# Moving subtractions of a sum of rows to GpSimd, a shorter root, and a split last scaling in a fused decoder layer

## The chip, the cores and the metric
The kernel runs on one core of a Trainium2 chip. The metric is the device time in microseconds (us), the median of several executions. The engines are TensorE (PE; its weight loads are listed as PEld), VectorE (DVE), ScalarE (ACT), GpSimd (POOL) and SyncE (SP), whose queue issues the transfers.

## The reference
One layer of a decoder over 16 meta tokens and 1024 tokens of width 1024. Only the second half of it and its norms matter here.

```python
def rmsnorm(x, g):
    x32 = x.astype(jnp.float32)
    y = x32 * lax.rsqrt(jnp.mean(x32 * x32, axis=-1, keepdims=True) + EPS)
    return (y * g.astype(jnp.float32)).astype(x.dtype)

def swiglu(u, w_gate, w_up, w_down):
    return (jax.nn.silu(u @ w_gate) * (u @ w_up)) @ w_down
...
        h = h + hybrid_mixer(rmsnorm(h, attn_norm_g[l]), pos, topk, w_in[l], mla_q_norm_g[l], w_uq[l],
                             mla_kv_norm_g[l], w_ukv[l], w_o[l])
        h = h + swiglu(rmsnorm(h, ffn_norm_g[l]), w_gate[l], w_up[l], w_down[l])
    h = rmsnorm(h, final_norm_g)
    return h[:, N_META:t]
```

The mixer holds two groups of attention heads (one dense, one over the 256 best keys of each query), and an output projection `w_o`. Norms are taken of the input, of two latent vectors, of the sum after the mixer, and of the result.

## The kernel before, in words
The 1024 tokens are eight blocks of 128 rows. Every float32 factor of a product is cut into a high part of fewer bits (written by ACT, `split`, line 188) and a low part, the difference of the factor and its high part (a subtraction on DVE or POOL, lines 191 and 193); a product is three matmuls (lines 196 to 198: high x high, high x low, low x high, in the order that the factors' roles give).

The stages in time order: the input norm and projection; the dense and the sparse attention for blocks 0 to 2 and then 3 to 7; the output projection of blocks 0 to 2 and their feed-forward part, inside the attention of the later blocks; the output projection of blocks 3 to 7 (`out_proj`); the feed-forward part of blocks 3 to 7 (`ffn_sums`); the last norm (`last_norm`) of each block as its last feed-forward sum comes in.

The feed-forward part of blocks 3 to 7 uses a scheme of seven products instead of eight quarter products. It works on sums of row halves and of column halves. `sums_of` writes the seven left factors `us[0]` to `us[6]` for each block from the block's two transposed halves, which lie in PSUM (`x11`, `x12`, `x21`, `x22`, 128 x 256 each); `first_factors` writes the weights' factors. The tiles `wsh` and `wsl` and parts of older tiles (`ckH`, `wkH`) are the slots for the high and low parts of these; of the seven, two low parts are subtracted by DVE and five by POOL.

`out_proj` goes over the blocks with a lag: after a block's projection comes the sum of its squares, the norm's factor (`rstd`, lines 155 to 161: six DVE instructions around one square root on ACT), two scaled halves `un` (line 1069), eight transposes on TensorE (line 1072), and then `put`, the sums of that block (lines 1107 to 1118), one block behind. The first transfers of the feed-forward weights go into four buffers `raw`; a buffer is loaded anew when the last reader of its contents is done.

`rstd` serves all norms: 9 at the input, 17 for the latent vectors, one call for blocks 0 to 2 together (three columns), 5 for blocks 3 to 7 and 8 for the last norm. In the last norm the first half of a block is scaled by DVE with the norm's factor and the weights at once (line 1301), the second half by ACT and then by POOL (lines 1298 and 1299), except for the last block, where DVE scales both halves.

The program text gives the work and what depends on what. In which order each engine's queue takes its instructions is written by a planner that simulates the whole program (`schedule_with_timeline_sim=True`); each queue then runs in that order.

Of the kernel before, what the change touches and what calls it, by code (L numbers as in the profile page):

```python
# [11 lines left out]
F32 = mybir.dt.float32  # L12
# [6 lines left out]
AF = mybir.ActivationFunctionType  # L19
OP = mybir.AluOpType  # L20
# [5 lines left out]
D = 1024  # L26
P = 128
NB = T // P
# [12 lines left out]
EPS = 1e-6  # L41

NA = 3
BLK_A, BLK_B = tuple(range(NA)), tuple(range(NA, NB))
# [33 lines left out]
SEG = P // 2  # L78
NSEG = NB - NA
NPR = 7  # L80
WS_N, RAW_N = 5, 4
# [24 lines left out]
def hybrid_layer(ctx, tc, a, out):  # L106
    nc = tc.nc
    V, S, G, PE = nc.vector, nc.scalar, nc.gpsimd, nc.tensor
    ld = nc.sync.dma_start
# [38 lines left out]
    def bcast_rows(src, n, parts=P):  # L148
        return bass.AP(tensor=src.tensor, offset=src.offset, ap=[[0, parts], [1, n]])

    def rstd(pool, ss, n, parts=P, tag="rs"):

        w = ss.shape[-1]
        v = pool.tile([parts, 4, w], F32, name=tag, bufs=3)
        V.tensor_scalar(v[:, 0], ss, 1.0 / n, EPS, op0=OP.mult, op1=OP.add)
        S.activation(v[:, 1], v[:, 0], AF.Sqrt)
        V.reciprocal(v[:, 1], v[:, 1])
        V.tensor_mul(v[:, 2], v[:, 1], v[:, 1])  # L158
        V.tensor_mul(v[:, 2], v[:, 2], v[:, 0])
        V.tensor_scalar(v[:, 2], v[:, 2], -0.5, 1.5, op0=OP.mult, op1=OP.add)  # L160
        V.tensor_mul(v[:, 3], v[:, 1], v[:, 2])
        return v[:, 3]

    def v_scale(pool, i, bound, rest):
# [21 lines left out]
    def split(h, l, src, eng=None):  # L186

        S.activation(h, src, AF.Copy)  # L188
        if eng is G and len(src.shape) == 2:
            for c in cuts(src.shape[-1], 256):  # L190
                G.tensor_sub(l[:, c], src[:, c], h[:, c])  # L191
        else:
            (eng or V).tensor_sub(l, src, h)  # L193
# [46 lines left out]
    with ExitStack() as es:  # L240
# [29 lines left out]
        def norm_in(src, parts, dst, t=-1):  # L270

            xt = xp.tile([P, D], F32, name="xt", bufs=2)
            ld(xt[:parts], src)
            if parts == NM:
                ld(gb, bcast_rows(a["attn_norm_g"], D))
            ss = xp.tile([P, 1], F32, name="ss", bufs=3)
            S.activation(act_junk()[:parts, :D], xt[:parts], AF.Square, accum_out=ss[:parts])
            r = rstd(xp, ss[:parts], D, parts, tag="rs")
            if t >= XT_G:
                S.activation(xt, xt, AF.Copy, scale=r)  # L280
                G.tensor_mul(xt, xt, gb)
            else:
                V.scalar_tensor_tensor(xt[:parts], xt[:parts], r, gb[:parts], op0=OP.mult, op1=OP.mult)
            for g in range(2):
                pt = ps_t()
                for d in range(4):
                    PE.transpose(pt[:, d * P:d * P + parts], xt[:parts, (g * 4 + d) * P:(g * 4 + d + 1) * P],
                                 ident[:parts, :parts])
                dst(slice(g * 4, g * 4 + 4), pt.rearrange("p (c n) -> p c n", n=P))
# [224 lines left out]
        def latent(dst, src, n, g, parts=P):  # L514
            ss = ip.tile([P, 1], F32, name="ssc", bufs=3)[:parts]
            S.activation(act_junk()[:parts, :n], src, AF.Square, accum_out=ss)
            r = rstd(ip, ss, n, parts, "rsc")
            V.scalar_tensor_tensor(dst, src, r, g[:parts], op0=OP.mult, op1=OP.mult)
# [141 lines left out]
    oh = [op.tile([P, D], F32, name=f"oh{t}") for t in range(NB)]  # L660
# [365 lines left out]
    def out_proj(wo, blocks, load, cw, ot, put, tps, ops, ends, lag=0):  # L1026
# [19 lines left out]
        for c, i in steps:  # L1046
# [15 lines left out]
            tot = wo.tile([P, 4], F32, name="ss2", bufs=2)[:, 0:i + 1 - i0]  # L1062
            V.reduce_sum(tot, ss[:, i0:i + 1], axis=AX.X)
            r = rstd(wo, tot, D, P, "rs2")
            for k in range(i0, i + 1):
                for g in range(2):
# [21 lines left out]
    def sums_of(wo, us):  # L1088

        def ot(i, part, g):
            return us[2 * part + g][:, i].rearrange("p a d n -> p (a d n)").rearrange("p (d n) -> p d n", n=P)

        first = {}

        def put(i, g, pt):
            if not g:
                first[i] = pt
                return  # L1100
            (x11, x12), (x21, x22) = ([x[:, :, j * SEG:(j + 1) * SEG] for j in range(2)] for x in (first.pop(i), pt))
            t0, t1, t2, t3, t4 = (wo.tile([P, 4, SEG], F32, name=f"ts{x}", bufs=1) for x in range(5))

            def parts(k, src, eng=None):
                split(us[k][:, i, 0], us[k][:, i, 1], src, eng)

            S.activation(t0, x11, AF.Copy)
            parts(0, x11)
            V.tensor_sub(t1, x12, t0)
            parts(1, x21)  # L1110
            V.tensor_sub(t2, x22, t1)
            parts(2, t2)
            parts(3, t1, G)
            G.tensor_sub(t3, t2, t0)
            parts(4, t3, G)
            parts(5, x22)
            V.tensor_sub(t4, x21, t2)
            parts(6, t4, G)

        return ot, put  # L1120
# [157 lines left out]
    def last_norm(fu):  # L1278

        gl = fu.tile([P, D], F32, name="gl")  # L1280
        ld(gl, bcast_rows(a["final_norm_g"], D))
        sums = {}

        def half(t, c):
            if not c:
                sums[t] = fu.tile([P, 2], F32, name="ss3", bufs=3)
            S.activation(fu.tile([P, 512], BF, name="yj"), oh[t][:, c * 512:(c + 1) * 512], AF.Square,
                         accum_out=sums[t][:, c:c + 1])
            if not c:
                return  # L1290
            tot = fu.tile([P, 1], F32, name="ss4", bufs=3)
            V.tensor_add(tot, sums[t][:, 0:1], sums[t][:, 1:2])
            r = rstd(fu, tot, D, P, "rs3")
            for k in range(2):
                y = oh[t][:, k * 512:(k + 1) * 512]
                g = gl[:, k * 512:(k + 1) * 512]
                if k and t < NB - 1:
                    S.activation(y, y, AF.Copy, scale=r)
                    G.tensor_mul(y, y, g)
                else:  # L1300
                    V.scalar_tensor_tensor(y, y, r, g, op0=OP.mult, op1=OP.mult)  # L1301
                ld(out[0, t * P:(t + 1) * P, k * 512:(k + 1) * 512], y)

        return half

    def pool(es, name, **kw):
        return es.enter_context(tc.tile_pool(name=name, bufs=1, **kw))
# [7 lines left out]
    with aa_es:  # L1315
        work = attention(aa, BLK_A, cfg)
        rest = mla_rest()
        n = 0
# [42 lines left out]
    fu = pool(fa, "fua")  # L1361
# [14 lines left out]
    for x, y in ((ckH, ckL), (wkH, wkL)):  # L1376
        n = x.shape[1] // WO_W
# [55 lines left out]
```

## Time and profile before
| what | us |
|---|---|
| runs: median (lowest, highest) of 3 | 1507.58 (1507.29, 1510.57) |
| the profiled execution | 1510.57 |
| its span, first to last instruction | 1508.8 |
| TensorE busy | 1403.7 |
| VectorE busy | 1101.3 |
| ScalarE busy | 923.7 |
| GpSimd busy | 893.6 |

The time of an execution holds its span and what lies around it. Busy times overlap. The granted clock is the share of TensorE's full rate that the chip granted; over the whole span it was 0.974.

### The profile page before, as it was taken

Reading aid. Unit: us, or ns where it says so; the run is one execution under the profiler, and the core shown is the slowest. Engines: PE = TensorE matmul, PEld = TensorE weight load, DVE = VectorE, ACT = ScalarE, POOL = GpSimd, SP = SyncE. Lnnn points to the kernel's source line nnn. Section 1 sums busy time; section 2 is a strip of 40 time slices with the busy share of each in tenths; the row PEclk is TensorE's granted clock in tenths of the full one; section 3 lists DMA queues with packets and bytes.
Section 4 is the critical chain, followed back from the end, with each engine's and each line's share of the span. In section 5 each row is a group of like instructions: output and inputs, shape, how many; then the busy total and the mean of one; then the engine's idle time right before and its main releaser. Section 6 shows DMA issues by size and latency. Waiting matters only on the chain. (4 is left out here: it accounts for less than half of the span.)

```text
span 1508.8 us, 29965 instructions
## 1 busy us (share of the span) xinstructions
PE 1403.7 (93%) x10320; PEld 1293.0 (86%) x10320; DVE 1101.3 (73%) x2714; ACT 923.7 (61%) x2264; POOL 893.6 (59%) x1185
## 2 busy tenths in 40 slices
PE   6999998899989799899999999897899999999996
PEld 5999998897879689798888888797899999999995
DVE  5888989948886785966776657647566777777766
ACT  5666678896888889788644444554544444444434
POOL 2573555212405587787878879663846666666653
PEclk9999999999999799999999999998899999999998
DMA  6213365223434788678879998661212222222211
GB/s 172 61 48 87 80 139 133 51 89 115 137 113 114 144 187 174 149 154 182 188 162 199 200 214 193 161 189 39 71 57 84 84 84 84 84 75 80 84 56 70
DMA packets 353737, 180.74 MB, mean 120 GB/s; under 512 B 196560, under 2 KB 341344, under 8 KB 353584
## 3 DMA queue, kind: packets, MB, share of 16 engines
q1 hardware_dynamic: 353584, 178.82, 48.0%
q8 instruction: 81, 1.33, 0.4%
q14 instruction: 72, 0.59, 0.1%
HBM read 120.77 MB, written 21.30 MB: 94 GB/s over the span
## 5 line engine op out<-in xcount | busy, mean ns | idle before, releaser
L191 POOL TENSOR_TENSOR wL<-raw,wH 128x256 fp32r<-128x256 f32 x352 | 286.7, 848 | 60.6 <-ACT wH L188 56.3
L821 POOL TENSOR_TENSOR hl<-pd,hl 128x260 f16<-128x260 f32 (+5 forms) x256 | 168.8, 689 | 70.5 <-ACT hl L817 38.0
L191 POOL TENSOR_TENSOR wsl<-raw,wsh 128x256 fp32r<-128x256 f32 x132 | 120.6, 942 | 95.9 <-ACT wsh L188 48.5
L196 PE MATMUL b<-wh,uH 128*128 128x256 f32 (+3 forms) x568 | 169.3, 298 | 5.1 <-DVE mlo L318 3.2
L198 PE MATMUL b<-wh,uL 128*128 128x256 f32 (+3 forms) x568 | 168.8, 298 | 0.0
L197 PE MATMUL b<-wl,uH 128*128 128x256 f32 (+3 forms) x568 | 168.5, 297 | 0.1
L188 ACT ACTIVATE wH<-raw 128x1024 fp32r<-128x1024 f32 x88 | 91.8, 1055 | 80.8 <-DMA raw<-in_w_gate 20.8
L196 PE MATMUL b<-us,wsh 128*128 128x320 f32 x440 | 136.2, 313 | 1.6 <-ACT us L188 1.0
L197 PE MATMUL b<-us,wsh 128*128 128x320 f32 x440 | 136.5, 311 | 0.4 <-DVE us L193 0.4
L198 PE MATMUL b<-us,wsl 128*128 128x320 f32 x440 | 134.8, 310 | 0.0
L196 PE MATMUL b<-ua,wH 128*128 128x384 f32 x352 | 121.8, 346 | 3.3 <-ACT wH L188 3.3
L382 ACT ACTIVATE js<-sc,bs 128x528 bf16<-128x528 int16 (+7 forms) x128 | 120.9, 944 | 4.8 <-DVE sc L437 2.4
L197 PE MATMUL b<-ua,wH 128*128 128x384 f32 x352 | 121.2, 344 | 0.0
L198 PE MATMUL b<-ua,wL 128*128 128x384 f32 x352 | 121.0, 345 | 0.0
L196 PE MATMUL b<-wH,hH 128*128 128x512 f32 x282 | 113.9, 404 | 4.4 <-ACT hH L188 3.1
L196 PEld LDWEIGHTS b<-wh,uH 128*128 128x128 f32 x568 | 108.8, 192 | 7.2 <-DVE mlo L318 3.9
L197 PE MATMUL b<-wL,hH 128*128 128x512 f32 x282 | 112.5, 399 | 0.0
L198 PE MATMUL b<-wH,hL 128*128 128x512 f32 x282 | 110.2, 400 | 0.4 <-DVE hL L193 0.4
L197 PEld LDWEIGHTS b<-wl,uH 128*128 128x128 f32 x568 | 109.1, 192 | 0.5 <-DVE wl L193 0.3
L198 PEld LDWEIGHTS b<-wh,uL 128*128 128x128 f32 x568 | 109.0, 192 | 0.4 <-DVE uL L193 0.2
L1248 DVE TENSOR_TENSOR oh<-b,oh 128x512 f32<-128x512 f32 x110 | 74.5, 685 | 43.3 <-PE b L198 42.6
L799 ACT ACTIVATE pd<-pd,sm 128x528 f32<-128x528 f32 (+4 forms) x80 | 75.7, 946 | 48.7 <-DVE sm L797 46.0
(410 smaller groups left out, 4834.9 us busy)
## 6 DMA issues: line engine op xcount, KB each, us to landing
raw<-in_w_gate SPq DMA_DIRECT2D x44, 512.0 KB, 4.0
raw<-in_w_up SPq DMA_DIRECT2D x44, 512.0 KB, 4.1
raw<-in_w_down SPq DMA_DIRECT2D x44, 512.0 KB, 3.6
wor<-in_w_o SPq DMA_DIRECT2D x64, 128.0 KB, 2.7
wraw<-in_w_in SPq DMA_DIRECT2D x40, 128.0 KB, 2.5
vh<-v_x SPq DMA_DIRECT2D x16, 288.0 KB, 4.0
xt<-in_x SPq DMA_DIRECT2D x8, 512.0 KB, 4.1
ks_x<-st SPq DMA_DIRECT2D x32, 128.0 KB, 2.2
```

Of the source, the lines that this page charges most:

```text
L188: S.activation(h, src, AF.Copy)
L191: G.tensor_sub(l[:, c], src[:, c], h[:, c])
L196: PE.matmul(o, lh, rh, start=first, stop=False, **kw)
L197: PE.matmul(o, lh, rl, start=False, stop=False, **kw)
L198: PE.matmul(o, ll, rh, start=False, stop=last, **kw)
L382: S.activation(act_junk()[:, :n_keys(b)], y[b], AF.Sign, bias=cols[0], accum_out=cnt)
L799: S.activation(pb, pb, AF.Exp, bias=mn, scale=-1.0, accum_out=z)
L821: G.tensor_sub(pl_[:, c], pb[:, c], ph[:, c])
L1248: V.tensor_add(oh[t][:, cs], po, oh[t][:, cs])
```

## The change
In `put`, the low part of `us[2]` is subtracted by POOL instead of DVE, in all five blocks. For blocks 3 to 6 (not the last) ACT copies `x22` from PSUM into a new tile `ts5`, both parts of `us[5]` are taken from this copy, and the low part is subtracted by POOL.

`rstd` takes -4 (mean + eps), its root with the sign turned in ACT's instruction, the reciprocal, and then one step of refinement in two DVE instructions if there is one column (three if there are more), where it took four.

In the last norm the last block's halves are multiplied by the norm's weights into a buffer of the `raw` ring (DVE: 512 and 256 columns, POOL: 256), ahead of the norm's factor; then DVE scales one half and ACT the other.

```diff
     def rstd(pool, ss, n, parts=P, tag="rs"):
 
+
         w = ss.shape[-1]
         v = pool.tile([parts, 4, w], F32, name=tag, bufs=3)
-        V.tensor_scalar(v[:, 0], ss, 1.0 / n, EPS, op0=OP.mult, op1=OP.add)
-        S.activation(v[:, 1], v[:, 0], AF.Sqrt)
+        V.tensor_scalar(v[:, 0], ss, -4.0 / n, -4.0 * EPS, op0=OP.mult, op1=OP.add)
+        S.activation(v[:, 1], v[:, 0], AF.Sqrt, scale=-1.0)
         V.reciprocal(v[:, 1], v[:, 1])
-        V.tensor_mul(v[:, 2], v[:, 1], v[:, 1])
-        V.tensor_mul(v[:, 2], v[:, 2], v[:, 0])
-        V.tensor_scalar(v[:, 2], v[:, 2], -0.5, 1.5, op0=OP.mult, op1=OP.add)
-        V.tensor_mul(v[:, 3], v[:, 1], v[:, 2])
+        if w == 1:
+            V.scalar_tensor_tensor(v[:, 2], v[:, 1], v[:, 1], v[:, 0], op0=OP.mult, op1=OP.mult)
+        else:
+            V.tensor_mul(v[:, 2], v[:, 1], v[:, 1])
+            V.tensor_mul(v[:, 2], v[:, 2], v[:, 0])
+        V.scalar_tensor_tensor(v[:, 3], v[:, 2], 3.0, v[:, 1], op0=OP.add, op1=OP.mult)
         return v[:, 3]
...
             V.tensor_sub(t2, x22, t1)
-            parts(2, t2)
+            parts(2, t2, G)
             parts(3, t1, G)
             G.tensor_sub(t3, t2, t0)
             parts(4, t3, G)
-            parts(5, x22)
+            if i < len(BLK_B) - 1:
+                t5 = wo.tile([P, 4, SEG], F32, name="ts5", bufs=1)
+                S.activation(t5, x22, AF.Copy)
+                x22 = t5
+            parts(5, x22, G if i < len(BLK_B) - 1 else V)
             V.tensor_sub(t4, x21, t2)
             parts(6, t4, G)
...
             if not c:
                 return
+            if t == NB - 1:
+
+                yg = fu.tile([P, D], F32, name="raw", bufs=RAW_N)
+                V.tensor_mul(yg[:, 0:512], oh[t][:, 0:512], gl[:, 0:512])
+                G.tensor_mul(yg[:, 512:768], oh[t][:, 512:768], gl[:, 512:768])
+                V.tensor_mul(yg[:, 768:], oh[t][:, 768:], gl[:, 768:])
             tot = fu.tile([P, 1], F32, name="ss4", bufs=3)
             V.tensor_add(tot, sums[t][:, 0:1], sums[t][:, 1:2])
             r = rstd(fu, tot, D, P, "rs3")
             for k in range(2):
+                if t == NB - 1:
+                    y = yg[:, k * 512:(k + 1) * 512]
+                    if k:
+                        S.activation(y, y, AF.Copy, scale=r)
+                    else:
+                        V.tensor_scalar(y, y, r, None, op0=OP.mult)
+                    ld(out[0, t * P:(t + 1) * P, k * 512:(k + 1) * 512], y)
+                    continue
                 y = oh[t][:, k * 512:(k + 1) * 512]
                 g = gl[:, k * 512:(k + 1) * 512]
-                if k and t < NB - 1:
+                if k:
                     S.activation(y, y, AF.Copy, scale=r)
                     G.tensor_mul(y, y, g)
                 else:
```

## Rows read from the trace of the kernel before
**Rows 1.** The page: span, and busy time of each engine (x instructions).
```profile
span 1508.8 us, 29965 instructions
...
PE 1403.7 (93%) x10320; PEld 1293.0 (86%) x10320; DVE 1101.3 (73%) x2714; ACT 923.7 (61%) x2264; POOL 893.6 (59%) x1185
```
**Rows 2.** Windows: start:end, length, busy time of each engine; clock, DMA share, GB/s.
```profile
100.00:200.00 100.00, 99.01 (x708) 97.54 (x707) 90.48 (x289) 68.25 (x205) 52.80 (x69) 1.00 0.35 91
1043.40:1061.00 17.60, 6.47 (x26) 4.17 (x27) 16.68 (x41) 9.41 (x30) 10.63 (x13) 0.60 0.09 31
1046.00:1068.80 22.80, 13.15 (x63) 11.13 (x62) 16.94 (x42) 13.40 (x37) 16.58 (x23) 0.63 0.07 24
1057.00:1068.80 11.80, 10.37 (x53) 9.25 (x52) 6.05 (x15) 7.29 (x18) 8.89 (x14) 0.70 0.00 1
1094.80:1474.00 379.20, 379.18 (x2210) 349.07 (x2211) 267.02 (x390) 157.92 (x309) 228.15 (x260) 1.00 0.26 77
```
**Rows 3.** TensorE's waits from 1000 us: who waited, total, times, longest.
```profile
PE b L1072 <- DVE un L1069: 7.1, 2, 3.7
PE b L196 <- ACT hH L188: 3.1, 1, 3.1
PE b L1072 <- DVE rs L160: 1.5, 1, 1.5
```
**Rows 4.** Groups by form, 1030 to 1066 us, and one tile's instructions (min/median/max).
```profile
L193 DVE TENSOR_TENSOR us<-b,us 128x256 fp32r<-128x256 f32 x15 | 6.2, 413 | 1.2 <-ACT us L188 1.2
L193 DVE TENSOR_TENSOR us<-ts,us 128x256 fp32r<-128x256 f32 x5 | 2.8, 551 | 1.0 <-ACT us L188 1.0
...
L193 POOL TENSOR_TENSOR us<-ts,us x15: 724/735/1267, 1033.5 to 1066.7; 128x256 fp32r<-128x256 f32 x15
...
L1107 ACT ACTIVATE ts<-b 128x256 f32<-128x256 f32 x5 | 1.8, 370 | 0.2 <-PE b L1072 0.2
```
**Rows 5.** Timeline of DVE, 1049 to 1056 us: start, length, instruction.
```profile
1050.44 0.88 DVE L193 TENSOR_TENSOR us<-ts,us 128x256 fp32r<-128x256 f32 x1
1051.24 0.41 DVE L193 TENSOR_TENSOR us<-b,us 128x256 fp32r<-128x256 f32 x1
...
1054.58 0.41 DVE L193 TENSOR_TENSOR us<-ts,us 128x256 fp32r<-128x256 f32 x1
1054.91 0.41 DVE L193 TENSOR_TENSOR us<-b,us 128x256 fp32r<-128x256 f32 x1
```
**Rows 6.** Timelines of POOL, SyncE's queue and DVE: the chain behind 1061 us.
```profile
1067.39 1.44 POOL L191 TENSOR_TENSOR wsl<-raw,wsh 128x256 fp32r<-128x256 f32 x2
...
1068.86 0.38 SPq L1192 DMA_DIRECT2D raw<-in_w_gate  x1
...
1091.58 0.69 DVE L1199 TENSOR_TENSOR sc<-raw 128x512 f32<-128x512 f32 x1 [4.06 <-DMA raw<-in_w_up]
```
**Rows 7.** Timelines of DVE, POOL and ACT in the tail, after TensorE's end.
```profile
1499.51 0.68 DVE L1248 TENSOR_TENSOR oh<-b,oh 128x512 f32<-128x512 f32 x1
...
1502.63 1.03 DVE L158 TENSOR_TENSOR rs<-rs 128x1 f32<-128x1 f32 x1
1503.69 0.16 DVE L159 TENSOR_TENSOR rs<-rs 128x1 f32<-128x1 f32 x1
1503.88 0.15 DVE L160 TENSOR_SCALAR rs<-rs 128x1 f32<-128x1 f32 x1
1504.07 0.16 DVE L161 TENSOR_TENSOR rs<-rs 128x1 f32<-128x1 f32 x1
1504.27 1.41 DVE L1301 SCALAR_TENSOR_TENSOR oh<-oh,rs,gl 128x512 f32<-128x512 f32 x2
...
1502.38 1.26 POOL L1299 TENSOR_TENSOR oh<-oh,gl 128x512 f32<-128x512 f32 x1 [1.48 <-ACT oh L1298]
...
1501.58 0.72 ACT L1298 ACTIVATE oh<-oh,rs 128x512 f32<-128x512 f32 x1 [0.29 <-DVE rs L161]
```
**Rows 8.** Timeline of DVE at the start, the first full block's norm.
```profile
10.45 0.16 DVE L161 TENSOR_TENSOR rs<-rs 128x1 f32<-128x1 f32 x1
10.64 1.29 DVE L283 SCALAR_TENSOR_TENSOR xt<-xt,rs,gb 128x1024 f32<-128x1024 f32 x1
```

## The prediction
> **What bounds the kernel now.** I read the page first. TensorE is busy for 93% of a span of 1508.8 us [rows 1], so a faster VectorE (DVE) instruction counts only where TensorE stands still. The windows show where that is. From 1094.8 us to 1474 us TensorE works 379.18 of 379.20 us, and from 100 to 200 us, where the 17 norms of the latent vectors are computed, 99.01 of 100 [rows 2]: an edit on another engine can move nothing there. From 1043.4 to 1061 us TensorE works only 6.47 of 17.6 us, at a mean granted clock of 0.60, while DVE works 16.68 [rows 2]. This is the end of the second output projection, with the norms of blocks 3 to 7 and the sums of rows (`put`). The list of TensorE's waits names the cause: transposes of `un` wait 7.1 us for DVE's `un`, 1.5 us more for a norm step [rows 3]. So DVE sets the time of this stretch.
>
> The next thing to see is what stands behind it. After 1061 us TensorE has one wait worth naming, 3.1 us at 1094.8 us, for the first hidden block `hH` [rows 3]. It comes down a chain of its own: GpSimd (POOL) ends its low parts of the first weight factors at 1068.8 us, only then does SyncE's queue issue the next `w_gate` load (1068.86 us), its factors keep DVE busy, a `w_up` load follows, and DVE stands 4.06 us in line for it at 1091.58 us [rows 6]; `hH` is queued behind. TensorE's total after 1094.8 us is fixed, so an earlier start at 1060 us is kept only as far as this chain starts earlier too. Last I read the timeline of the tail, a serial chain on DVE and ScalarE (ACT) [rows 7].
>
> **The sums of rows, the largest part.** Per block `put` loses on DVE the low part of `us[2]` (two SBUF inputs) in all five blocks and that of `us[5]` (one input in PSUM) in four. These instructions last 0.551 and 0.413 us on average [rows 4]; back to back they take the time to the next start: 1054.58 to 1054.91, so 0.33 us, but 1050.44 to 1051.24, so 0.80, where POOL was running [rows 5]. Before the last `un` (block 7, issued at 1055.6 us) lie both instructions of blocks 4 and 5: 0.80 + 0.33 + 2 x 0.33 = 1.8 us. Two steps fewer in the norms of blocks 6 and 7 would be 4 x 0.19 = 0.8 us by the distance of such steps [rows 7]; some of them run in the shadow of other work, and I take 0.5 us. Together 2.3 us of DVE.
>
> What it adds: nine subtractions on POOL, 0.735 us median, 0.724 to 1.267 [rows 4], four copies on ACT at the 0.37 us of the `ts` copy [rows 4], and 0.04 us each where ACT's high part of `us[5]` now waits for that copy. ACT works 9.41 of 17.6 us in the stretch [rows 2], so I cost the copies at nothing; without that cover they would cost 4 x 0.37 = 1.5 us. POOL's nine come where DVE has instructions with two SBUF inputs, and the trace shows what meeting does: DVE's `us<-ts` takes 0.41 us alone, 0.88 with POOL running [rows 4, 5], POOL's 0.72 becomes 1.27 [rows 4]. DVE instructions with one PSUM input stay at 0.41. The Trainium skill ("SBUF — State Buffer", section "Who interferes with whom") has the rule: a DVE instruction with two SBUF inputs and a GpSimd instruction that reads SBUF share a port pair by an exclusive lock, and the second one waits in full. The trace agrees, 0.88 beside 0.41. By that rule every meeting costs, which would take the start below to 0.4 us earlier and the sum at the end to 1506.1 us; by the rows only some instructions meet, and the sum stays.
> DVE's two `un` per block still have two SBUF inputs; of the four added POOL instructions of blocks 4 and 5 I let one in three cost DVE the 0.47 us between 0.88 and 0.41, 0.6 us. Bounds: none (0), or all four (1.9). So TensorE's products start 2.3 - 0.6 = 1.7 us earlier (0.4 to 2.3).
>
> Does POOL let that through? From 1057 to 1068.8 us it works 8.89 of 11.8 us [rows 2], 2.9 idle. Three of the new instructions (block 6's two, block 7's one) fall here: 3 x 0.735 = 2.2 us, which would fit, but some of the idle time is waiting for ACT's high parts. If all fit, the weights' low parts end 1.7 us earlier; if none, 0.5 later. I take 1.2 earlier: most of them fit, since ACT is half idle. SyncE's `w_gate` load, and with it the whole chain to `hH`, moves by the same. So this part gives **1.2 us** (bounds: 2.3 gained, 0.5 lost).
> "GPSIMD Engine Reference" of the Trainium skill (section "Engine selection") says elementwise work does not belong on GpSimd, about twice as slow as VectorE with two inputs. The rows show 0.735 beside 0.41 [rows 4], 1.8 times. The rule by itself would make this part a loss. It would be right if POOL were the bound; that is the last rival below.
>
> **The root.** With one column (39 of 40 calls) six DVE instructions become four: the factor -4 goes into the first and into ACT's sign scale (free, the same instruction), and two `scalar_tensor_tensor` replace four. The trace has no 128x1 instruction of that form; the neighbours are 0.16 to 0.17 us and start 0.19 apart [rows 7]. It cannot be cheaper than those, and DVE's `un` of the same form takes what its elements take, so I use 0.19, with 0 and 0.3 as bounds. Each chain gets 0.38 us shorter. It counts where TensorE waits on it: at the start the second tile's norm ends at 10.64 us in steps of 0.19 [rows 8], but weights are still being loaded and cut, so I take half, 0.2 us (0 to 0.4). The group of three blocks keeps three multiplications and loses one step, 0.2. In the latents: nothing (cover: TensorE's 99%); without it, 17 x 0.38 = 6.5 us of DVE. Block A's last norms (975 to 992 us): 0.1. Sum **0.5 us** (0 to 0.9).
>
> **The tail.** After TensorE's end, block 7 now goes: reciprocal, first multiplication 1502.63 (1.03 us, held up by POOL's multiplication for block 6, 1502.38 to 1503.64), then 1503.69, 1503.88, 1504.07, then two scalings one after the other from 1504.27, 1.41 us [rows 7]. After: the first new instruction meets the same POOL instruction, the second follows at 1503.69, scaling starts at 1503.88. The gain `g` has been multiplied in before, so one half goes to DVE, the other to ACT, side by side. DVE's half has one SBUF input; bounds 0.41 (256 columns, [rows 4]) to 0.75 (its older form). ACT takes 0.72 [rows 7] and sets the end: 1504.60 where it was 1505.68. **1.1 us**. What it adds ahead of that: products of 512 and 256 columns on DVE (0.75 by the older form [rows 7], 0.41 by the 256-column subtraction [rows 4]) and one of 256 columns on POOL (0.735), which fit between the last eviction and the norm's factor, where DVE waits for ACT. If DVE takes the first ahead of the last eviction (1499.51 us), 0.75 us is lost; if fewer norm steps also let evictions go earlier, up to 0.7 more is won. Bounds 0.3 and 1.8. The output transfers are the same sixteen.
>
> **Sum.** 1.2 + 0.5 + 1.1 = 2.8 us. The profiled execution took 1510.57 us around its span of 1508.8; the median of the runs shown is 1507.58, 2.99 lower, and these terms are subtracted from that: **1504.8 us**. The program's order is written by a planner that simulates the whole, so each edit also moves instructions that it doesn't touch; the rivals hold that.
>
> **Rivals.**
> *A new order that helps.* DVE's 4.06 us in line for `w_up` [rows 6] is a matter of order: `hH`'s inputs were there. If the planner puts them first, TensorE's 3.1 us goes: 1504.8 - 3.1 = 1501.7 us. For it: each time around it moves; against: nothing in the change aims there.
> *The early start is swallowed.* The chain through `w_gate` stays where it is, TensorE's wait at 1094.8 us grows from 3.1 to 4.8. Left are root and tail: 1507.58 - 1.6 = 1506.0 us. For it: POOL's order decides, DVE's saving lies before it.
> *A new order that hurts.* One more wait like the 3.1 us opens elsewhere: 1507.9 us.
> *POOL becomes the bound, slower.* Seven of the new instructions lie between 1046 and 1068.8 us, where POOL works 16.58 of 22.8 us [rows 2]. If its 6.2 idle us are all dependency waits, it ends 5.1 us (at 0.735) to 8.9 us (at 1.267) later against 1.7 from the earlier start; with root and tail (1.6) that is +1.8 to +5.6, in the middle 1511.3 us. The products of `us[2]` would wait for POOL. It decides against the change from 3.3 us of unabsorbed POOL time on; by 0.2% from 6.3.
>
> **How the numbers follow.** A change of 0.2%, 3.0 us, is about what can be told from none. Chances: the forecast 0.45 (its own range 1503.2 to 1506.3, 0.22 of it below 1504.56), help 0.23, swallowed 0.12, hurt 0.08, POOL 0.12. Faster: 0.22 + 0.23 = 0.45; same: 0.23 + 0.12 + 0.04 (half of hurt) = 0.39; slower: 0.12 + 0.04 = 0.16. The range reaches into both: 1501.0 to 1510.0, leaving out the far part of help (0.07) and most of POOL (0.1).
>
> **What would show it.** Right: products start near 1058 us; DVE's `us<-ts` gone and nine more on POOL, near 0.74 us; the 128x1 steps four per norm; last scaling within 0.75 us. Wrong: POOL without gaps from 1050 us and TensorE waiting for its `us`; a longer wait for `hH`; the 128x1 `scalar_tensor_tensor` above 0.3 us; block 7's product with `g` ahead of the last eviction; new waits in the attention part.

## The result, and the profile after

The changed kernel takes **1522.11 us** (median of four runs, 1520.20 to 1526.13) beside 1508.95 for the kernel before (four runs, 1507.29 to 1510.57): a ratio of 1.009, 95% interval 1.0068 to 1.0113. It is slower by about 13 us, outside the range that was given. The execution that was profiled took 1526.13 us.

The page of the kernel after, which answers to [rows 1]:
```profile
span 1524.3 us, 29895 instructions
...
PE 1408.2 (92%) x10320; PEld 1296.8 (85%) x10320; DVE 1104.9 (72%) x2627; ACT 928.1 (61%) x2269; POOL 893.2 (59%) x1195
```
DVE has 87 instructions fewer and POOL 10 more, as the change says. No engine works much more; the span is 15.5 us longer. The next two views cut it into stages. The cuts lie at 480 and 740 us, at the end of the first feed-forward half (the last product with `ua`), at the first product of the sums `us`, at the last product with `hH`, and at the end. Columns: stretch, length, TensorE's busy time (products), its granted clock, DMA share, GB/s. Before:
```profile
0.00:480.00 480.00, 438.86 (x3420) 0.98 0.38 103
480.00:740.00 260.00, 239.17 (x1986) 0.96 0.77 165
740.00:963.90 223.90, 212.76 (x1797) 0.99 0.86 185
963.90:1059.80 95.90, 80.02 (x618) 0.92 0.44 127
1059.80:1498.10 438.30, 432.07 (x2506) 0.99 0.25 75
1498.10:1508.80 10.70, 0.77 (x4) 0.63 0.45 173
```
After:
```profile
0.00:480.00 480.00, 434.50 (x3404) 0.98 0.38 103
480.00:740.00 260.00, 240.75 (x1978) 0.95 0.75 165
740.00:968.30 228.30, 214.11 (x1751) 0.99 0.82 178
968.30:1072.80 104.50, 86.82 (x690) 0.92 0.46 127
1072.80:1511.40 438.60, 431.26 (x2506) 0.99 0.25 74
1511.40:1524.30 12.90, 0.75 (x4) 0.69 0.43 163
```
The products of the sums, which `put` was to bring forward, begin 13.0 us later (1072.8 for 1059.8). The long stretch behind them is as long as before (438.6 for 438.3), and the tail takes 2.2 us more. So 13 of the 15.5 us are lost ahead of `put`'s products. There, length minus busy time gives TensorE's idle time: 89.0 us before, 96.6 after, 7.6 more. The other 5.4 us are longer busy time for the same number of products. Of these the granted clock makes some 2 us by estimate (its mean up to the sums is 0.970 before and 0.968 after, over 1073 us); the rest isn't explained. Over the kernels below this busy time goes from 967.5 to 977.1 us without following their times. The idle time is what follows them.

Where does TensorE stand still? The list of its waits over the whole span of after, the lines that bear on it and that answer to [rows 3]:
```profile
PE b L1075 <- DVE un L1072: 8.2, 3, 7.1
PE b L199 <- DVE vw L171: 5.2, 1, 5.2
PE b L199 <- DVE oh L1059: 4.7, 5, 2.3
...
PE b L199 <- ACT oh L1230: 3.9, 1, 3.9
...
PE b L199 <- ACT hH L191: 2.1, 1, 2.1
PE b L201 <- POOL wL L194: 1.9, 3, 1.4
```
The wait for `vw` (a scale of the value columns), at 291.9 us, was 0.3 us before. The wait for `un` was 8.6 with its norm step [rows 3], 9.7 with a second norm step of 1.1 that those rows leave out, and is 8.2 now. Of the wait for `oh` of L1059, 4.0 us lie in the output projection, where 2.7 us for `woh` stand beside it; neither is in the list of this stage before. Behind the sums 3.9 us for `oh` of L1230 stand in place of the 3.1 for `hH`. The waits for `hH` and `wL` here lie in the first feed-forward half, where before had none of these above 0.4. From 200 to 320 us idle time is 3.7 us longer, from 740 us to the sums 4.9. None of these longer waits is for a tile that the diff writes otherwise.

**The second place.** ACT searches the keys that block 7, the last block, attends to; block 7 can't start until that is done. The search closes with two small steps on POOL, and then DVE takes over. The timelines of ACT, POOL and DVE before, at the end of block 7's first search:
```profile
662.66 0.29 ACT L383 ACTIVATE bs<-bs,th 128x1 f32<-128x1 f32 x1
...
663.88 0.21 POOL L389 TENSOR_SCALAR bs<-bs 128x1 f32<-128x1 f32 x1
664.18 0.19 POOL L390 TENSOR_TENSOR bs<-bs 128x1 f32<-128x1 f32 x1
...
664.41 1.30 DVE L436 TENSOR_SCALAR_CACHE_REDUCE jk<-sc,bs 128x1040 bf16<-128x1040 int16 x1
```
From ACT's last step to DVE's it takes 1.75 us. The same steps after:
```profile
684.40 0.29 ACT L386 ACTIVATE bs<-bs,th 128x1 f32<-128x1 f32 x1
...
688.11 0.53 POOL L392 TENSOR_SCALAR bs<-bs 128x1 f32<-128x1 f32 x1
688.59 5.60 POOL L194 TENSOR_TENSOR wL<-raw,wH 128x256 fp32r<-128x256 f32 x8
694.15 0.19 POOL L393 TENSOR_TENSOR bs<-bs 128x1 f32<-128x1 f32 x1
...
699.30 1.29 DVE L439 TENSOR_SCALAR_CACHE_REDUCE jk<-sc,bs 128x1040 bf16<-128x1040 int16 x1
```
Now it takes 14.9 us. POOL's queue holds eight pieces of weights (5.60 us) between the two steps, others ahead of the first, and DVE's queue holds other work ahead of its own. This delay is one part of three: ACT's last step itself comes 21.7 us later (684.40 for 662.66), these steps add 13.2, and the second search, behind them, takes 17.8 less (56.8 for 74.6 from its first comparison to its last). It starts its last comparison at 758.7 us where it was 741.9. TensorE's value products (`pT`) of block 7 pause until 800.3 us where it was 781.3. Windows of these products, columns as above, first before and then after:
```profile
780.00:800.00 20.00, 3.06 (x81) 1.00 0.83 182
...
780.00:800.00 20.00, 0.00 (x0) 1.00 0.36 88
```
TensorE fills the gap with the feed-forward half, and then that filler is used up: 90 value products stand behind its end, where 27 did. What comes behind them, the output projection and all after it, has less beside it to cover its waits. By the two views of the stages 3.1 of the 4.9 us are lost ahead of the feed-forward half's end and 1.8 behind it, so the missing filler is not the whole of it.

In the tail, answering to [rows 7], DVE after:
```profile
1512.68 0.68 DVE L1301 TENSOR_TENSOR raw<-oh,gl 128x512 f32<-128x512 f32 x1
...
1513.42 0.68 DVE L1255 TENSOR_TENSOR oh<-b,oh 128x512 f32<-128x512 f32 x1
...
1515.54 1.21 DVE L1305 TENSOR_TENSOR ss<-ss 128x1 f32<-128x1 f32 x1
...
1517.11 0.75 DVE L1322 SCALAR_TENSOR_TENSOR oh<-oh,rs,gl 128x512 f32<-128x512 f32 x1
...
1517.97 1.22 DVE L160 SCALAR_TENSOR_TENSOR rs<-rs 128x1 f32<-128x1 f32 x1
...
1519.42 0.48 DVE L1313 TENSOR_SCALAR raw<-raw,rs 128x512 f32<-128x512 f32 x1
```
The product with `g` stands ahead of the last eviction (1513.42, DVE taking the last product out of PSUM), and two 128x1 steps take 1.2 us each, while POOL multiplies. From the end of the last eviction to the end of the span it was 8.6 us and is 10.2. Of this 1.0 us lies behind the last scaling: from its end (ACT, 1520.20 us) to the end of the span it takes 4.1 us where it was 3.1. SyncE's queue after shows 0.6 us of it:
```profile
1520.36 0.38 SPq L1323 DMA_DIRECT2D out_y<-oh  x1
1520.83 0.39 SPq L1314 DMA_DIRECT2D out_y<-raw  x1
```
The last half, ready at 1520.20, is issued at 1520.83, behind the first half and a transfer of block 6. Before, it was issued at 1505.71, where its scaling ended at 1505.68.

### The profile page after: what moved, and what is told of

The parts are those of the page before. It is cut to its first block, busy times and chain, and to the rows that moved or that the text cites. A ratio compares the mean times of both kernels' runs of the same rounds, so it can differ in the third digit from the quotient of the medians.

```text
span 1524.3 us, 29895 instructions
## 1 busy us (share of the span) xinstructions
PE 1408.2 (92%) x10320; PEld 1296.8 (85%) x10320; DVE 1104.9 (72%) x2627; ACT 928.1 (61%) x2269; POOL 893.2 (59%) x1195
## 4 chain that ended last, share of the span: by engine, by line
PE 52%; DVE 17%; DMA 11%; POOL 8%; issue 6%; ACT 6%; SPq 0%; POOLq 0%; ACTq 0%; DVEq 0%
PE b L199 14%; PE b L201 14%; PE b L200 14%; DMA pT<-hl 4%; POOL wL L194 4%; PE b L793 3%; DVE jk L400 3%; POOL hl L824 2%; DMA raw<-in_w_gate 1%; DMA raw<-in_w_up 1%; DMA wraw<-in_w_in 1%; DVE pd L795 1%; DVE sc L364 1%; ACT js L385 1%; DVE bs L409 1%
```

## The experiments

The theory after the first reading: the short root in the early norms changes the simulated times, so the planner writes other queues, and those cost the time. The rivals: the sums on POOL cost it; the new tail does; or the new instructions of the root are slow themselves.

One table holds what the fourteen profiles say of the stage ahead of the sums. Columns: start of the second search's last comparison; value products behind the feed-forward half's end; start of the sums' products; TensorE's idle time up to there (from windows, as above).

| kernel | search | behind | sums | idle |
|---|---|---|---|---|
| before | 741.9 | 27 | 1059.8 | 89.0 |
| after | 758.7 | 90 | 1072.8 | 96.6 |
| root_only | 752.0 | 90 | 1064.5 | 96.2 |
| put_only | 739.5 | 27 | 1059.6 | 88.9 |
| last_only | 742.3 | 27 | 1063.2 | 88.1 |
| late_root | 741.2 | 27 | 1057.3 | 83.8 |
| root_lat | 757.1 | 105 | 1066.4 | 98.9 |
| root_in | 753.9 | 105 | 1064.6 | 94.5 |
| plac_a | 738.7 | 27 | 1057.9 | 87.5 |
| idle_four | 759.5 | 105 | 1071.0 | 93.9 |
| fixs_after | 743.1 | 27 | 1061.8 | 91.5 |
| fixs_before | 749.1 | 0 | 1069.8 | 99.6 |
| put_late | 744.5 | 27 | 1061.0 | 86.7 |
| put_late_l2 | 739.6 | 27 | 1058.9 | 84.9 |

The six kernels with 93.9 us of idle time or more are those that lose 8 us or more in the median. Their idle time is 4.9 to 10.6 us above before's, six to nine tenths of what they lose in the median; the rest isn't placed, since one execution of each was profiled.

The order itself can be read by comparing each engine's instructions one by one with before's. In late_root, put_late and put_late_l2 all four engines run in before's order to 977 us, in put_only to 1034: as far as the edit begins. In after, root_only, root_in and idle_four TensorE's order, whose instructions no edit touches, parts from it at 30 us, in plac_a at 55, in root_lat at 118.

**root_only.** Of the diff only the part in `rstd`.
```diff
-        V.tensor_mul(v[:, 2], v[:, 1], v[:, 1])
...
+            V.scalar_tensor_tensor(v[:, 2], v[:, 1], v[:, 1], v[:, 0], op0=OP.mult, op1=OP.mult)
...
+        V.scalar_tensor_tensor(v[:, 3], v[:, 2], 3.0, v[:, 1], op0=OP.add, op1=OP.mult)
```


> The root in four operations in all 40 calls; the sums of rows and the last scaling as before. Theory O (order): the shorter root shifts the planner's simulated times from the first norm on, the queues through the attention stages come out in another order, block 7's selection of keys ends some 16 us later and TensorE has 90 rows of value products left (27 before) when the feed-forward part of blocks 0 to 2 ends; this alone costs the whole loss and somewhat more, 12 to 15 us over the kernel before. Theory P (POOL is the bound of the sums of rows): the root is a gain, 0 to 1 us faster than before.

1519.18 us beside 1508.78, ratio 1.0077 (1.0058 to 1.0096): 10.4 us, a little under the 12 to 15 expected. The root alone makes most of the loss. Block 7's step takes 15.1 us here (679.38 to 694.48), with the same eight pieces between, and the wait for `vw` is 5.1.

**put_only.** Of the diff only the part in `put`.
```diff
-            parts(2, t2)
+            parts(2, t2, G)
...
+                S.activation(t5, x22, AF.Copy)
+                x22 = t5
+            parts(5, x22, G if i < len(BLK_B) - 1 else V)
```


> Only the low parts of us[2] and us[5] go to POOL. The queues are those of before up to about 1030 us. Theory O: the products of the second feed-forward part start earlier and the time is 0.5 to 2.5 us under the kernel before. Theory P: POOL has no gaps from 1046 us on, TensorE waits for its low parts, and the time is 5 to 13 us over the kernel before.

1506.27 beside 1508.78, ratio 0.9995 (0.9976 to 1.0013): not to be told from no change (its twelve runs spread from 1502.75 to 1517.48). Its queues up to the output projection are those of before. The groups by form, 1030 to 1066 us (columns as in [rows 4]), show what the subtractions did on DVE:
```profile
L1070 DVE SCALAR_TENSOR_TENSOR un<-oh,rs,gbf 128x512 f32<-128x512 f32 x8 | 8.6, 1110 | 0.1
L160 DVE TENSOR_TENSOR rs<-rs 128x1 f32<-128x1 f32 x4 | 2.3, 575 | 0.0
```
Before, these were 868 ns (6.7 us in all) and 330 ns (1.3). So `un` and one norm step together took 2.9 us more in this stretch (a second norm step 0.7 more), against the 4.4 us that the nine removed subtractions had lasted (2.8 and 4 x 0.413, [rows 4]).

**last_only.** Of the diff only the part in the last norm.
```diff
+                V.tensor_mul(yg[:, 0:512], oh[t][:, 0:512], gl[:, 0:512])
+                G.tensor_mul(yg[:, 512:768], oh[t][:, 512:768], gl[:, 512:768])
...
+                        S.activation(y, y, AF.Copy, scale=r)
...
+                        V.tensor_scalar(y, y, r, None, op0=OP.mult)
```


> Only the last block's scaling on two engines, with the old root. Queues as before except at the very end. Both theories: 0.5 to 1.2 us faster, because two scalings of 0.7 us go side by side; if the product with the weights goes ahead of the last eviction on VectorE, no gain.

1508.92 beside 1508.78, ratio 1.0000 (0.9986 to 1.0014). From the end of the last eviction (1501.35) to the end of the span (1511.5) it takes 10.1 us, 8.6 before [rows 7]; from TensorE's end, 10.9 for 9.9. The part gains nothing where it was to gain.

**late_root.** The whole change, but the norms at the input, of the latents and of the group of three keep the old root. Against after:
```diff
+        if tag in ("rs", "rsc") or w > 1:
+            V.tensor_scalar(v[:, 0], ss, 1.0 / n, EPS, op0=OP.mult, op1=OP.add)
...
+            V.tensor_mul(v[:, 3], v[:, 1], v[:, 2])
+            return v[:, 3]
```


> The whole change, but the input norms, the latent norms and the norm of blocks 0 to 2 keep the old root; the short one serves the norms of blocks 3 to 7 and the last norm. Theory O: the order through the attention stages is that of before, and the time is 2 to 4 us under the kernel before. Theory P: as slow as the whole change, 10 to 15 us over the kernel before.

1505.69 beside 1508.78, ratio 0.9984 (0.9968 to 0.9999). With the early norms as they were, the whole loss is gone, though both other parts are in.

**root_lat** and **root_in.** The short root in the 17 norms of the latents alone, or in the 9 at the input alone; all else as before.
Against root_only, whose edit each cuts down:
```diff
+        if tag != "rsc":
+            V.tensor_scalar(v[:, 0], ss, 1.0 / n, EPS, op0=OP.mult, op1=OP.add)
...
+            return v[:, 3]
```
```diff
+        if tag != "rs":
+            V.tensor_scalar(v[:, 0], ss, 1.0 / n, EPS, op0=OP.mult, op1=OP.add)
...
+            return v[:, 3]
```


> The short root only in the 17 latent norms, all else as before. TensorE is fully busy there, so the shorter root itself is worth nothing. Theory O: the queues come out in another order behind it (105 rows of value products left at the end of the feed-forward part of blocks 0 to 2, 27 before; POOL's two steps at the end of the search for block 7 lie apart, with 8 pieces of other work between them); 8 to 15 us slower than before. Rival S (the short root's instructions are slow themselves, or delay a stage that matters): within 2 us of before, since this stage has cover.

> The short root in the 9 input norms alone. Theory O: the queues come out with 105 rows of value products behind the feed-forward part (27 before), POOL's two search steps for block 7 apart by 8 pieces of other work; 8 to 15 us slower than before. Rival: only the latent norms' shift matters, then within 2 us of before or up to 0.4 us faster from the start.

root_lat 1520.13 beside 1508.09, ratio 1.0074 (1.0056 to 1.0093); root_in 1517.54 beside 1508.45, 1.0066 (1.0045 to 1.0087). Either alone loses about as much as both: the loss is no sum over instructions. root_in's idle time from 200 to 320 us is as before (10.6 for 10.1), and 4.2 of its 5.5 us of added idle time lie between 740 us and the sums, so the search and what follows suffice for a loss.

**plac_a** and **idle_four.** Before, with the old root and all arithmetic; behind it one idle instruction in the 9 input norms, or four in each of the 26 input and latent norms. They write a column that nobody reads any more.
```diff
         V.tensor_mul(v[:, 3], v[:, 1], v[:, 2])
+        if tag == "rs":
+            V.memset(v[:, 0], 0.0)
```
```diff
         V.tensor_mul(v[:, 3], v[:, 1], v[:, 2])
+        if tag in ("rs","rsc"):
+            for _ in range(4):
+                V.memset(v[:, 0], 0.0)
```


> The kernel before with one idle VectorE instruction (a memset of one column that nobody reads) behind each of the 9 input norms; nothing is left out. VectorE's and ScalarE's queues come out in another order, TensorE's keeps 27 rows of value products behind the feed-forward part and POOL's two search steps stay together. Theory O in its narrow form (the place of these steps costs): within 2 us of before. Theory O in its wide form (any other order costs, before was a lucky one): 5 us or more slower.

> The kernel before, its old root, with four idle VectorE instructions (memsets of one column that nobody reads) behind each of the 26 input and latent norms. 104 of them at 59 ns are 6 us of VectorE, in stages where TensorE was busy for 99 of 100 us or waits for weights, so by themselves worth 0 to 3 us. The planner answers them with the order that the short root got in the input or latent norms alone: 105 rows of value products behind the feed-forward part, the same eight pieces of work between POOL's two steps for block 7. Theory O: block 7's selection ends 12 to 16 us later than before and the time is 8 to 16 us over it. If the loss belongs to the root's own instructions: 0 to 3 us over it.

plac_a 1507.36 beside 1508.09, ratio 0.9999 (0.9983 to 1.0016). idle_four 1518.11 beside 1510.13, 1.0046 (1.0028 to 1.0063). Both add work to the early norms; only one loses. plac_a's POOL runs in before's order to the end. idle_four's order is like root_in's at the search: POOL's queue there
```profile
686.26 0.22 POOL L393 TENSOR_SCALAR bs<-bs 128x1 f32<-128x1 f32 x1
686.43 2.38 POOL L825 TENSOR_TENSOR hl<-pd,hl 128x228 f16<-128x228 f32 x4
688.76 2.80 POOL L195 TENSOR_TENSOR wL<-raw,wH 128x256 fp32r<-128x256 f32 x4
691.50 0.52 POOL L394 TENSOR_TENSOR bs<-bs 128x1 f32<-128x1 f32 x1
```
holds eight other instructions between the two steps, and its DVE step follows at 697.19, 15.9 us after ACT's at 681.25. The 104 idle instructions are not the cost themselves: idle time up to 200 us grew by 1.7 us, from 200 to 320 us it shrank by 1.3, and from 740 us on it grew by 3.6. This speaks against slow new instructions as the cause: there are none in this kernel.

**fixs_after** and **fixs_before.** In after, and in before as a control, the two steps that close the search are one DVE instruction.
```diff
-                G.tensor_scalar(up, up, 0.5, None, op0=OP.mult)
-                G.tensor_sub(cols[1], up, cols[0])
+                V.scalar_tensor_tensor(cols[1], up, 0.5, cols[0], op0=OP.mult, op1=OP.subtract)
```


> The whole change, and the end of each ScalarE search (two POOL instructions on one column) is one VectorE instruction instead. If the wait of these steps in POOL's queue is what delays block 7 (14.9 us from the search's last count to the next VectorE step where it was 1.8), the loss goes: 0 to 4 us under the kernel before. If the delay comes from the order of the queues as such, 8 us or more over it remain.

> The kernel before with the end of each search on VectorE, the control for the last one. Before, the two steps were hardly held up in POOL's queue for block 7, so within 3 us of before if only their wait matters.

fixs_after 1511.68 beside 1508.09, ratio 1.0025 (1.0007 to 1.0043): of 13 us some 4 are left, where 0 to 4 under before were expected if the wait was the cause, and 8 or more over it if the order as such was. Neither came. The search ends at 743.1 and 27 value products are left behind, as before the change; from 740 us to the sums TensorE idles 24.7 us, for 31.9 in after. This edit too rewrites the queues: ACT's last step of the first search, ahead of the edited place, comes at 665.5 us, 18.9 earlier than in after. So it shows that the loss leaves with the late search, not that this one wait is worth 9 us.

The control missed: fixs_before takes 1520.21 beside 1508.09, ratio 1.0080 (1.0061 to 1.0099), where no more than 3 us of difference were expected. Its TensorE queue parts from before's at 233 us, far ahead of block 7's search. It leaves no value product behind, but of its 10.6 us of added idle time 5.5 lie from 480 to 740 us (2.9 from 200 to 320), the longest single wait there being
```profile
PE b L199 <- DVE hL L194: 5.0, 1, 5.0
```
The edit that goes with a better order in one kernel goes with a worse one in the other. What it costs here is a matter of the order that comes out, not of the place that was edited.

**put_late** and **put_late_l2.** The sums on POOL and the short root in the late norms only, with the old last scaling; and the same with a smaller change of the last scaling, where only the second half is multiplied by `g` ahead. Against late_root, and then against put_late:
```diff
-                yg = fu.tile([P, D], F32, name="raw", bufs=RAW_N)
-                V.tensor_mul(yg[:, 0:512], oh[t][:, 0:512], gl[:, 0:512])
...
-                        S.activation(y, y, AF.Copy, scale=r)
...
-                        V.tensor_scalar(y, y, r, None, op0=OP.mult)
```
```diff
+            if t == NB - 1:
+                yg = fu.tile([P, D], F32, name="raw", bufs=RAW_N)[:, 512:]
+                V.tensor_mul(yg, oh[t][:, 512:], gl[:, 512:])
...
+                if k and t == NB - 1:
+                    S.activation(y, yg, AF.Copy, scale=r)
```


> The sums of rows as in the change and the short root for the norms of blocks 3 to 7 and the last norm; old root in the early norms, old last scaling. Theory: the two parts that are worth something, without the order's loss and without the split scaling, whose product with the weights goes ahead of the last eviction. 3 to 5 us under the kernel before; from the last eviction to the end of the span 8.2 us (8.6 before, 10.2 with the split scaling).

> As the last one, and of the last block only the second half is multiplied by the weights ahead of the norm's factor, on VectorE, from the half that the last eviction writes (so it cannot go ahead of that), then scaled by ScalarE while VectorE scales the first half as before. If the order of VectorE's queue was what cost the split scaling its gain, the tail from the last eviction is 7.5 to 7.8 us and the time 4 to 6 us under the kernel before; if GpSimd's port or the transfers set the end, 8.2 us or more.

put_late: 1504.11 beside 1508.45, ratio **0.9966** (0.9951 to 0.9981), faster than both kernels. put_late_l2: 1504.82, ratio 0.9969 (0.9956 to 0.9983), no better, where 4 to 6 us under before were expected. From the last eviction to the end put_late takes 8.2 us; put_late_l2 takes 8.8, where 7.5 to 7.8 were expected. DVE in the tail of put_late_l2:
```profile
1496.68 1.16 DVE L1312 TENSOR_TENSOR raw<-oh,gl 128x512 f32<-128x512 f32 x1 [0.40 <-DVE rs L167]
...
1499.25 1.03 DVE L169 SCALAR_TENSOR_TENSOR rs<-rs 128x1 f32<-128x1 f32 x1
```
The product comes behind the eviction (1495.53 us) this time, but takes 1.16 us, and the norm's step after it 1.03, both beside POOL's multiplications. Its two scalings end together (1501.26 and 1501.29 us), their transfers are issued one after the other (1501.29, 1501.71), and 3.7 us pass from there to the end, 3.1 in put_late.

## Why the prediction was wrong

**The step that failed** is in the root: "In the latents: nothing (cover: TensorE's 99%)". As a count of the instructions' own time it holds: from 100 to 200 us TensorE works 99.06 us after, 99.01 before [rows 2]. But the root was given 0 to 0.9 us of gain, and root_only measured 10.4 us of loss. The instructions of the input's and the latents' norms stand early, and with an edit there the queues of all that follows come out in another order: root_lat, root_in and idle_four show it with three different edits, and late_root, in before's order to 977 us, shows that without it the loss is gone.

**The sentence that should have caught it** was there: "each edit also moves instructions that it doesn't touch; the rivals hold that." They held it with a wrong price. *A new order that hurts* was one more wait like the 3.1 us at the end of the kernel, with a chance of 0.08. A new order from the start moves many waits at once, and cost 8 to 12 us in the median in root_only, root_lat, root_in, idle_four and fixs_before. "New waits in the attention part" was named among the signs of a wrong prediction, without a time.

**The sums of rows.** The count was right: DVE's `us<-ts` are gone and POOL has nine more, at 0.736 us median, as the tile's row of after shows:
```profile
L196 POOL TENSOR_TENSOR us<-ts,us x24: 719/736/1187, 1046.9 to 1080.7; 128x256 fp32r<-128x256 f32 x24
```
That they would bring the start forward was not: in put_only it came 0.2 us earlier. What each edit does at this place can be read more closely, since TensorE's last 200 products ahead of the sums are the same in every kernel and begin with the same one. From the start of that one to the start of the sums, in before, put_only, root_only and late_root:
```profile
1022.20:1059.82 37.62, 26.74 (x203) 0.83 0.11 36
1021.90:1059.64 37.74, 26.96 (x202) 0.85 0.12 36
1029.21:1064.51 35.30, 26.30 (x202) 0.88 0.13 39
1021.16:1057.32 36.16, 26.92 (x202) 0.86 0.12 37
```
The kernels with neither edit here have 37.60 to 37.62 us, those with both (after too) 36.15 to 36.18. So the start did come 1.5 us earlier, near the 1.7 that was forecast (0.4 to 2.3), but by luck: the two steps fewer per norm, taken as 0.5, are worth 2.3 alone, and the subtractions, taken as 1.2, lose 0.1 alone and 0.9 beside the short root. How the norms' steps come to 2.3 us was not followed.

The step that fell short in the subtractions is the meetings, "one in three cost DVE the 0.47 us": not only `us`, but `un` and the 128x1 steps met POOL's work, 2.9 us in two of the groups. Had all four of the counted instructions met, the prediction's 1.8 - 1.9 would have given 0.1 us later, as put_only measured. The rule of the Trainium skill ("SBUF — State Buffer", "Who interferes with whom"), by which every meeting costs, is that case. The trace is nearer to the rule than to my share. In the whole kernel the part is at most a small gain. *POOL becomes the bound* is refuted by put_only: from the sums' first product to the last with `hH` it takes 436.4 us, 438.3 before. The 3.1-us wait for `hH` is gone there and in put_late, whose longest wait behind the sums is 1.2 us, for `ckH`. That is *a new order that helps*, in the kernels that have the subtractions on POOL and keep the early norms: 434.4 us in put_late and late_root. (put_only's 436.4 alone says less: last_only, in before's order up to there, has 436.5.) In after it did not come: SyncE issues the next `w_gate` load at 1082.83 us, 10.0 behind the first product of the sums, where it was 9.1 [rows 6].

**The root where it counts.** Ahead of the sums it gives 2.3 us by itself, as said. In the tail of root_only it gives 0.4 us from the last eviction on (8.2 for 8.6), as "Each chain gets 0.38 us shorter" had it. But the eviction itself comes later: it ends 2.2 us behind TensorE's last product, 1.3 in before, because a scaling ahead of it
```profile
1501.71 1.87 DVE L1304 SCALAR_TENSOR_TENSOR oh<-oh,rs,gl 128x512 f32<-128x512 f32 x1
```
now starts with POOL's multiplication of 1501.74 us (1.29 us) and takes 1.87 us instead of 0.75. From TensorE's end the tail is 0.4 us longer (10.3 for 9.9), in root_only and in put_late. At the start the scaling of the first full block begins at 10.50 us in after and 10.60 in root_only, 0.14 and 0.04 earlier than in [rows 8]. A 128x1 `scalar_tensor_tensor` takes 0.14 to 0.22 us alone, near the 0.19 that was taken.

**The tail.** Forecast was a gain of 1.1 us with a lower bound of 0.3. last_only lost 1.5 us from the last eviction on, after 1.6 (from TensorE's end 1.0 and 2.3). The case that was named for the bound came true, DVE took the product with `g` ahead of the last eviction, and two things that were not counted came on top: POOL's new product and its old ones hold up the 128x1 steps on which the chain hangs, and the transfers, "the same sixteen", end 0.35 us (last_only) to 1.0 us (after) further behind the last scaling.

**Sum.** Of the 15.5 us between the two profiles 7.6 are idle time ahead of the sums, 5.4 longer busy time there (some 2 of it the clock), 0.3 the long stretch, 2.2 the tail. In the medians 13.2 us are lost; how much of them goes to the clock isn't known, since one execution of each kernel is profiled.

**What stays open.** Why the planner finds one order and not the other was not looked into, nor could any run hold the order fixed and change the instructions alone. So it is shown that early edits of either sign cost time together with a new order, and that the loss is gone where the old order stays, but not how much each wait costs. For the wait for `vw` no experiment was made by itself, and half of fixs_before's added idle time is placed (480 to 740 us) but not traced to one instruction.

## What to carry to other kernels

Where a simulation writes the queues, an edit early in the program is a new draw of the order of everything behind it; here that cost 8 to 12 us for a forecast of 0.5, in five of the six kernels that edit before early (plac_a lost nothing). Make such edits where little comes behind them, compare the order of all queues with the old one before believing any sum of durations, and put a few idle instructions at the same place to see what order alone can cost. An instruction that moves to GpSimd is not gone for VectorE: count what the two do at the same time. And where two edits meet at one place, measure each alone: here one's gain hid the other's loss.

## What the runs showed of the hardware

A VectorE instruction on 128x1 with two inputs in SBUF can be held up as long as GpSimd goes on: alone it takes 0.14 to 0.22 us, beside one 1.26-us multiplication 1.22, and in fixs_after, beside a queue of GpSimd work without a gap, 7.37:
```profile
665.85 7.37 DVE L392 SCALAR_TENSOR_TENSOR bs<-bs 128x1 f32<-128x1 f32 x1 [2.49 <-ACT bs L386]
```
with GpSimd's timeline beside it:
```profile
666.06 0.75 POOL L194 TENSOR_TENSOR ckL<-wor,ckH 128x256 fp32r<-128x256 f32 x1
666.75 3.04 POOL L823 TENSOR_TENSOR hl<-pd,hl 128x264 f16<-128x264 f32 x5
669.73 2.79 POOL L194 TENSOR_TENSOR wL<-raw,wH 128x256 fp32r<-128x256 f32 x4
672.46 0.74 POOL L194 TENSOR_TENSOR ckL<-wor,ckH 128x256 fp32r<-128x256 f32 x1
```
It did not get in between two of them: it ended at 673.22 us, when the last of these eleven had (673.20). In after, two 128x4 `tensor_scalar` took 4.70 us together from 691.77 us; the first ended at 696.34, and GpSimd, at work without a gap until then, at 696.32. VectorE's scaling of 128x512 took 0.48 us as `tensor_scalar` (L1313 above) and 0.75 as `scalar_tensor_tensor` (L1322 above).
